# Two products of the mixing stage on GpSimd: the decay matrix times the B-C scores, and the normalisation of the probabilities

## The chip, the core and the metric

One core of a Trainium2 chip runs the whole program. The metric is the device time of one execution in microseconds (us); a kernel's time is the median of several executions. Engines are named as in the profile: PE is TensorE (matmuls; PEld its weight loads), DVE is VectorE, ACT is ScalarE, POOL is GpSimd, SP is SyncE, which issues most DMAs. L12 is line 12 of the kernel.

## What is computed

Two layers of a decoder trunk on 256 positions of width 1024. Each layer has a SwiGLU feed-forward half step, a mixing block, a second half step and a gated input embedding. The mixing block projects the normalised input and runs three branches: sparse attention over keys that an indexer picks, a pooling mixer, and a state-space scan in chunks of 128 (SSD). The two places that matter here, cut from the reference:

```python
# attention: per query block and head
logits = jnp.where(valid, q_lat @ c_sel * (HEAD_DIM ** -0.5), -jnp.inf)
probs = jax.nn.softmax(logits, axis=-1)

# SSD: per chunk, group and head
L = jnp.exp(segsum(A))                 # decay from position s to l, 0 above the diagonal
cb = jnp.einsum("bclgn,bcsgn->bgcls", Cc, Bc)
y_diag = jnp.einsum("bgecls,bcsgep->bclgep", cb[:, :, None] * L, X)
```

The normalisation of `probs` by its row sums is one of the two products, `cb * L` the other.

## The kernel before

Matmuls of float32 are done in three passes: each operand is split into a rounded high part and the rest. A weight tile of 128x1024 arrives by DMA on SP's queue as `raw` (4 buffers); ACT rounds it to `whi` (L145, 5 buffers); DVE subtracts, `wlo` = `raw` - `whi` (L146, 5 buffers); PE multiplies high by high, high by low and low by high (L211, L212, L213). Tiles are loaded in one fixed order, up to four ahead of the one in use, so ACT and DVE prepare weights all the time beside whatever else they do.

The mixing block (`mix`) writes its branches as generators and interleaves them with `weave`, which calls each generator in turn so that PE always has projection matmuls (the three branch gates `gates`, the pooling inputs) between the short steps of attention and SSD. A step of PE that needs a result is put some turns behind the step that makes it (the bare `yield`s). This gives the program order. The tile framework then plans the order of each engine's instructions by a timeline of its own (`schedule_with_timeline_sim=True` in `program`), except where the kernel fixes it (`keep_in_program_order` in `mm` and `transpose`, an order token in `turn`). So a change of an engine for some instructions can alter the order of others too. Waits between engines are semaphores, set by the framework from the tiles that are read and written.

The SSD branch (`ssd`) goes over 2 groups of 8 heads (g) and 2 chunks (h). For each it makes two tiles `m` of 128x512, four heads each (q): a scan on DVE adds up the decay rates (L1099), ACT takes the exponential (L1104), for h = 0 DVE copies the last column to `e0` (L1107), and DVE multiplies `m` by the masked scores `cb`, the same for the four heads (L1108). After three yields eight matmuls read the two tiles (`near`), in the profile `aux<-ct,ul`. That is four pairs of products per layer.

In attention, `softmax` works on two PSUM tiles of 128x512 at a time: four heads of 128 keys (first half of the queries), or two heads of 256 keys. For each head DVE adds the mask and takes the row minimum of the negated logits (L921); ACT takes the exponential and its row sum (L923); DVE takes the reciprocals (L925); ACT multiplies each head by its own (L927, four or two instructions per tile). After some yields PE transposes the probabilities (L114, `aux<-ident,t`), ACT copies them out of PSUM (L939), and the value matmuls read them. There are three rounds per layer, six tiles.

Other instructions that the prediction names: L1085, POOL's product of the SSD inputs with dt; L1030 and L1031, small DVE steps of dt; L1168 and L1169, DVE's sliding sums of the pooling branch; L1183, POOL's low part for one of the four pooling groups; L1153, DVE's multiply by the gate of SSD. The tiles of one tag share a name in the profile: `ct` is `m`, `gl` holds `cb` among others, `t` the probabilities.

Of the kernel before, what the change touches and what calls it, by code (L numbers as in the profile page):

```python
# [13 lines left out]
OP = mybir.AluOpType  # L14
AX = mybir.AxisListType

P = 128
# [51 lines left out]
class Builder:  # L69
# [838 lines left out]
    def softmax(self, h, two, mb, out):  # L908

        nc = self.nc  # L910
        nb = h + 1
        nk = nb * P
        per = 512 // nk
        prs = []
        for ps, _ in two:
            pr = self.t([P, per, nk])
            mx = self.t([P, per], tag="mx", bufs=2)
            sums = self.t([P, per], tag="sum", bufs=2)
            for j in range(per):
                x = mx[:, j:j + 1]  # L920
                nc.vector.tensor_tensor_reduce(pr[:, j], ps[:, j * nk:(j + 1) * nk], mb[:, :nk],  # L921
                                               1.0, 3.0e38, OP.add, OP.min, accum_out=x)
                self.last = nc.scalar.activation(pr[:, j], pr[:, j], AF.Exp, bias=x, scale=-1.0,  # L923
                                                 accum_out=sums[:, j:j + 1])
            nc.vector.reciprocal(sums, sums)  # L925
            for j in range(per):
                nc.scalar.mul(pr[:, j], pr[:, j], sums[:, j:j + 1])  # L927
            prs.append(pr)
            yield
        for _ in range(4 - h):  # L930
            yield
        pts = [self.bank("aux") for _ in prs]
        for pt, pr in zip(pts, prs):
            for j in range(4):
                self.transpose(pt[:, j * P:(j + 1) * P],
                               pr[:, j // nb, (j % nb) * P:(j % nb + 1) * P], self.ident)
        for (_, heads), pt in zip(two, pts):
            th = self.t([P, 4, P])
            nc.scalar.copy(th, pt.rearrange("p (a b) -> p a b", a=4))  # L939
            out.append((heads, th))  # L940
            yield
# [63 lines left out]
    def ssd(self, layer, sm, xs, xt, bc, cb, zs, room):  # L1005
        nc = self.nc
# [53 lines left out]
        def rate(*key):  # L1060
            i = wanted.index(key)
            for k in wanted[i:i + 3]:
                if k not in rates:
                    rates[k] = fetch(*k)
            return rates[key]
# [26 lines left out]
        for g in range(2):  # L1092
            gs = slice(g * 4, (g + 1) * 4)
            for h in range(2):
                ms = self.a([P, 2, 4, P], F, "ct")
                for q in range(2):

                    m = ms[:, q]
                    nc.vector.tensor_tensor_scan(m.rearrange("p a b -> p (a b)"),  # L1099
                                                 rate(g, h, q).rearrange("p a b -> p (a b)"),  # L1100
                                                 self.after.rearrange("p a b -> p (a b)"),
                                                 0.0, OP.add, OP.mult)
                    yield
                    self.last = nc.scalar.activation(m, m, AF.Exp)  # L1104
                    if h == 0:
                        k = g * 8 + q * 4
                        nc.vector.tensor_copy(e0[:, k:k + 4], m[:, :, P - 1])  # L1107
                    nc.vector.tensor_tensor(m, m, cb[:, h, g, None].to_broadcast([P, 4, P]),  # L1108
                                            op=OP.mult)
                    yield  # L1110
                ps = self.bank("aux")

                def near():
                    for j in range(8):
                        b, k = (j % 2) * 64, j // 2
                        self.mm(ps[b:b + 64, k * P:(k + 1) * P],
                                         xt[:, h, g * 8 + j], ms[:, j // 4, j % 4],
                                         start=True, stop=True)

                yield  # L1120
                yield
                yield near
                yk = y[:, gs, h * P:(h + 1) * P]
                nc.vector.tensor_tensor(yk, yk, ps.rearrange("p (a b) -> p a b", a=4), op=OP.add)
                yield

            x0 = self.t([P, 8, 64])
            nc.vector.tensor_tensor(x0, xt[:, 0, g * 8:(g + 1) * 8],
                                    e0[:, g * 8:(g + 1) * 8, None].to_broadcast([P, 8, 64]),
                                    op=OP.mult)  # L1130
            po = self.bank("aux")
            e1 = self.t([P, 4, P])
            x = rate(g, 1, 2)
            for j in range(4):
                nc.vector.tensor_tensor_scan(e1[:, j], x[:, j], self.ones, 0.0, OP.add, OP.mult)
            self.last = nc.scalar.activation(e1, e1, AF.Exp)
            yield
            yield
            for j in range(4):
                a = x0[:, 2 * j:2 * j + 2].rearrange("p a b -> p (a b)")  # L1140
                self.mm(po[:, j * P:(j + 1) * P], a, cb[:, 2, g], start=True, stop=True)
            yield
            nc.vector.tensor_tensor(e1, po.rearrange("p (a b) -> p a b", a=4), e1, op=OP.mult)
            yk = y[:, gs, P:]
            nc.vector.tensor_tensor(yk, yk, e1, op=OP.add)
            yield
            if g == 0:
                ysh, ysl = [], []
            ysh.append(self.a([P, 4, S], FR, "a4", 7))
            ysl.append(self.a([P, 4, S], FR, "a4", 7))  # L1150
            for i in range(4):
                k = g * 4 + i
                nc.vector.tensor_tensor(y[:, k], y[:, k], zs[:, k], op=OP.mult)  # L1153
                self.square(k, y[:, k])
                self.split_scaled(ysh[g][:, i], ysl[g][:, i], y[:, k],
                                  self.col(layer, "ssd_norm", k))
                yield
# [336 lines left out]
```

## Time and profile before

| | |
|---|---|
| median of 3 executions | 1299.63 us (1299.38 to 1300.03) |
| profiled execution | 1300.84 us, span 1299.1 us |
| granted PE clock | 1.0 throughout |
| DMA | 250.51 MB, mean 193 GB/s |
| POOL instructions | 27 |

The span is the time from the first to the last instruction of the profiled execution; its device time is 1.74 us longer. An engine's busy time is a sum over instructions, and matmuls overlap each other in the pipeline. In a row of a timeline the first number is the start, the second the duration of the piece, both in us; a bracket gives the idle time before it on its engine, and what ended that. A row of waits reads: engine and line that waited, engine and line waited for, us in total, times, longest. A row for a line gives durations in ns as minimum, median and maximum.

### The profile page before, as it was taken

How to read it: one execution, taken by the hardware profiler on the slowest of the kernel's cores; microseconds unless marked ns; L12 is line 12 of the kernel's file. 1: busy time of each engine (PE TensorE's matmuls, PEld its weight loads, DVE VectorE, ACT ScalarE, POOL GpSimd, SP SyncE). 2: the span in 40 equal slices, each digit the busy share in tenths (PEclk: the TensorE clock that was granted, in tenths of full speed). 3: DMA queues.
4: the chain of work that ended last, by engine and by line, in shares of the span. 5: the costliest groups of instructions: out<-in, count | busy, mean ns of one | idle time of the engine just before them, and what ended most of it. 6: DMA issues, size and time to landing. Idle time of an engine off the chain costs nothing.

```text
span 1299.1 us, 28286 instructions
## 1 busy us (share of the span) xinstructions
PE 1290.3 (99%) x11398; PEld 1282.0 (99%) x11398; DVE 1046.3 (81%) x1935; ACT 739.5 (57%) x1209; POOL 17.9 (1%) x27
## 2 busy tenths in 40 slices
PE   9999999999999999999999999999999999999998
PEld 9999999999999999999999999999999999999998
DVE  7877669987999887766997776799879989777667
ACT  6644446666874555544654444476667646544455
POOL 0000000000000000000000000000100000000000
PEclk9999999999999999999999999999999999999999
DMA  7766646586647576666556665556965566655661
GB/s 251 247 193 195 194 158 211 179 222 205 188 142 235 162 227 194 195 191 194 188 195 194 194 196 191 162 192 184 212 224 165 183 199 211 197 195 193 194 194 66
DMA packets 89571, 250.51 MB, mean 193 GB/s; under 512 B 25184, under 2 KB 27872, under 8 KB 89440
## 3 DMA queue, kind: packets, MB, share of 16 engines
q1 hardware_dynamic: 89008, 247.92, 60.6%
q8 instruction: 89, 1.46, 0.5%
q10 hardware_dynamic: 432, 0.79, 0.2%
q14 instruction: 42, 0.34, 0.1%
HBM read 245.50 MB, written 1.08 MB: 190 GB/s over the span
## 4 chain that ended last, share of the span: by engine, by line
PE 87%; DVE 7%; ACT 2%; DMA 2%; issue 2%; DVEq 0%; SPq 0%; ACTq 0%
PE mm L213 27%; PE mm L212 27%; PE mm L211 27%; DVE wlo L146 2%; DVE ct L1099 1%; PE aux L111 1%; ACT whi L145 1%; DMA gh<-rates 1%; DMA raw<-in_w_dram 1%; PE mm L230 1%; PE mm L227 1%; PE aux L213 1%; PE aux L212 1%; ACT t L923 1%; PE mm L225 1%
## 5 line engine op out<-in xcount | busy, mean ns | idle before, releaser
L145 ACT CAST whi<-raw 128x1024 fp32r<-128x1024 f32 (+1 forms) x456 | 475.1, 1045 | 484.9 <-PE mm L212 353.8
L146 DVE TENSOR_TENSOR wlo<-raw,whi 128x1024 fp32r<-128x1024 f32 (+1 forms) x456 | 552.2, 1215 | 170.1 <-ACT whi L145 162.2
L212 PE MATMUL mm<-ul,whi 128*128 128x256 f32 x2438 | 672.0, 276 | 0.0
L213 PE MATMUL mm<-uh,wlo 128*128 128x256 f32 x2438 | 671.8, 277 | 0.0
L211 PE MATMUL mm<-uh,whi 128*128 128x256 f32 x2402 | 662.3, 277 | 0.8 <-ACT whi L145 0.8
L212 PEld LDWEIGHTS mm<-ul,whi 128*128 128x128 f32 x2438 | 457.5, 188 | 0.1
L213 PEld LDWEIGHTS mm<-uh,wlo 128*128 128x128 f32 x2438 | 457.0, 188 | 0.2
L211 PEld LDWEIGHTS mm<-uh,whi 128*128 128x128 f32 x2402 | 449.8, 188 | 2.1 <-ACT whi L145 1.2
L213 PE MATMUL mm<-gh,wlo 128*128 128x256 f32 x704 | 194.1, 276 | 0.0
L212 PE MATMUL mm<-gl,whi 128*128 128x256 f32 x704 | 194.1, 276 | 0.0
L211 PE MATMUL mm<-gh,whi 128*128 128x256 f32 x704 | 193.7, 276 | 0.0
L213 PEld LDWEIGHTS mm<-gh,wlo 128*128 128x128 f32 x704 | 132.2, 188 | 0.0
L212 PEld LDWEIGHTS mm<-gl,whi 128*128 128x128 f32 x704 | 132.2, 188 | 0.0
L211 PEld LDWEIGHTS mm<-gh,whi 128*128 128x128 f32 x704 | 131.9, 188 | 0.0
L212 PE MATMUL mm<-a,whi 128*128 128x256 f32 x256 | 70.7, 276 | 0.0
L213 PE MATMUL mm<-a,wlo 128*128 128x256 f32 x256 | 70.7, 276 | 0.0
L211 PE MATMUL mm<-a,whi 128*128 128x256 f32 x256 | 70.7, 276 | 0.0
L213 PEld LDWEIGHTS mm<-a,wlo 128*128 128x128 f32 x256 | 48.1, 188 | 0.0
L211 PEld LDWEIGHTS mm<-a,whi 128*128 128x128 f32 x256 | 48.1, 188 | 0.0
L212 PEld LDWEIGHTS mm<-a,whi 128*128 128x128 f32 x256 | 48.1, 188 | 0.0
L498 DVE TENSOR_TENSOR t<-mm,rs_r 128x256 f32<-128x256 f32 x88 | 37.3, 424 | 13.2 <-PE mm L213 13.0
L499 DVE TENSOR_TENSOR t<-t,mm 128x256 f32<-128x256 f32 x87 | 36.5, 420 | 2.6
(300 smaller groups left out, 1271.1 us busy)
## 6 DMA issues: line engine op xcount, KB each, us to landing
raw<-in_w_dram SPq DMA_DIRECT2D x446, 512.0 KB, 4.3
gh<-rates SPq DMA_DIRECT2D x16, 256.0 KB, 4.1
raw<-in_w_dram SPq DMA_DIRECT2D x8, 352.0 KB, 3.0
ul<-a SPq DMA_DIRECT2D x32, 64.0 KB, 4.8
a<-in_x_dram SPq DMA_DIRECT2D x3, 512.0 KB, 5.3
gh<-rates SPq DMA_DIRECT2D x8, 128.0 KB, 4.5
a<-in_x_dram SPq DMA_DIRECT2D x1, 544.0 KB, 3.7
raw<-in_w_dram SPq DMA_DIRECT2D x2, 256.0 KB, 4.4
```

The costliest lines, as they stand in the source:

```text
L111: self.tc.keep_in_program_order(self.nc.tensor.matmul(*args, **kw))
L145: nc.scalar.copy(hi[:, :n], raw[:, :n])
L146: ins = nc.vector.tensor_tensor(lo[:, :n], raw[:, :n], hi[:, :n].bitcast(F), op=OP.subtract)
L211: (self.mm if keep else mm)(ps, a[0], b[0], start=start, stop=False)
L212: mm(ps, a[0], b[1], start=False, stop=False)
L213: mm(ps, a[1], b[0], start=False, stop=stop)
L225: (self.mm if keep and k == 0 else mm)(ps, w[0][:, s], u[0][:, k], start=k == 0, stop=False)
L227: mm(ps, w[0][:, s], u[1][:, k], start=False, stop=False)
L230: mm(ps, w[1][:, k * P:(k + 1) * P], u[0][:, k], start=False, stop=k == last)
L498: ins = [nc.vector.tensor_tensor(t, p1[0], r, op=OP.mult), nc.vector.tensor_tensor(g, t, p1[1], op=OP.mult)]
L499: nc.vector.tensor_tensor(g, t, p1[1], op=OP.mult)]
L923: self.last = nc.scalar.activation(pr[:, j], pr[:, j], AF.Exp, bias=x, scale=-1.0, accum_out=sums[:, j:j + 1])
```

## The change

Both products are given to POOL. In `softmax` one product per tile takes the place of four or two ACT multiplies: the reciprocals are spread over the keys by a stride of zero. In `ssd` only the engine changes. Nothing else in the code differs.

```diff
@@ softmax
             nc.vector.reciprocal(sums, sums)
-            for j in range(per):
-                nc.scalar.mul(pr[:, j], pr[:, j], sums[:, j:j + 1])
+            nc.gpsimd.tensor_tensor(pr, pr, sums[:, :, None].to_broadcast([P, per, nk]), op=OP.mult)
             prs.append(pr)
@@ ssd
                         nc.vector.tensor_copy(e0[:, k:k + 4], m[:, :, P - 1])
-                    nc.vector.tensor_tensor(m, m, cb[:, h, g, None].to_broadcast([P, 4, P]),
+                    nc.gpsimd.tensor_tensor(m, m, cb[:, h, g, None].to_broadcast([P, 4, P]),
                                             op=OP.mult)
```

## The prediction

> **What bounds the kernel now.** I read the page first (busy times, then the chain that ended last), then the waits of PE, then the busy time of each engine in stretches of the mixing stage, where both edits lie, and last the timeline of one stretch, engine by engine.
>
> ```profile
> span 1299.1 us, 28286 instructions
> PE 1290.3 (99%) x11398; PEld 1282.0 (99%) x11398; DVE 1046.3 (81%) x1935; ACT 739.5 (57%) x1209; POOL 17.9 (1%) x27
> PE 87%; DVE 7%; ACT 2%; DMA 2%; issue 2%; DVEq 0%; SPq 0%; ACTq 0%
> ```
>
> PE works through the whole span: 1299.1 - 1290.3 leaves 8.8 us in which it does nothing. Taking work off DVE or ACT can only give back what PE waits for them. The waits of PE and its weight loads that bear on this change are these three:
>
> ```profile
> PE mm L211 <- ACT whi L145: 0.8, 2, 0.5
> PE aux L114 <- ACT t L927: 0.8, 2, 0.4
> PEld mm L212 <- POOL t L1183: 0.4, 2, 0.2
> ```
>
> The mixing stage of each layer is the one place where DVE is full (columns: PE, PEld, DVE, ACT, POOL busy):
>
> ```profile
> 289.00:369.00 80.00, 79.35 (x740) 76.66 (x738) 69.53 (x154) 58.10 (x124) 6.13 (x5) 1.00 0.60 190
> 930.00:1010.00 80.00, 79.58 (x731) 77.12 (x731) 70.84 (x160) 57.77 (x124) 6.89 (x6) 1.00 0.63 197
> ```
>
> PE idles 0.65 us in the first of these stretches and 0.42 us in the second, 1.07 us together: all that the stage can give back, apart from small gaps between pipelined matmuls. DVE has 80 - 69.53 = 10.5 us free in the first one, but not evenly: in its middle it has none.
>
> ```profile
> 329.00:359.00 30.00, 30.00 (x298) 28.94 (x298) 29.97 (x66) 23.34 (x50) 1.22 (x1) 1.00 0.61 186
> ```
>
> **What is removed and added.**
>
> ```profile
> L1108 DVE TENSOR_TENSOR ct<-ct,gl x16: 684/692/699, 306.9 to 1002.5; 128x512 f32<-128x512 f32 x16
> L927 ACT ACTIVATE t<-t,sum x32: 389/450/507, 325.2 to 1005.1; 128x128 f32<-128x128 f32 x16, 128x256 f32<-128x256 f32 x16
> L925 DVE RECIPROCAL sum<-sum x12: 154/165/179, 323.2 to 1004.0; 128x2 f32<-128x2 f32 x8, 128x4 f32<-128x4 f32 x4
> L1085 POOL TENSOR_TENSOR ul<-ul,dt x8: 1036/1038/1905, 289.6 to 936.6; 128x512 f32<-128x512 f32 x8
> ```
>
> DVE loses 16 x 0.692 = 11.1 us, ACT 32 x 0.450 = 14.4 us. One reciprocal goes with one tile of probabilities, so POOL gains 12 products beside the 16: 28, or 14 per layer. L1085 is the same work, a product of 128x512 with a broadcast factor, on POOL already: 1.038 us at the median, so 29.1 us in all. POOL is idle 98% of the span, so its own time is no bound; the questions are when each product ends, and what its maximum of 1.905 us means:
>
> ```profile
> 289.60 4.91 POOL L1085 TENSOR_TENSOR ul<-ul,dt 128x512 f32<-128x512 f32 x4 [22.69 <-DMA raw<-in_w_dram]
> 289.27 0.19 DVE L1030 SCALAR_TENSOR_TENSOR dt<-dt_y,dt_x 128x32 f32<-128x32 f32 x1
> 289.38 1.23 DVE L146 TENSOR_TENSOR wlo<-raw,whi 128x1024 fp32r<-128x1024 f32 x1
> 290.52 1.03 DVE L1031 SCALAR_TENSOR_TENSOR da<-dt,al 128x32 f32<-128x32 f32 x1
> 937.17 1.58 DVE L146 TENSOR_TENSOR wlo<-raw,whi 128x1024 fp32r<-128x1024 f32 x1 [1.37 <-ACT whi L145]
> ```
>
> Four products at 1.038 would take 4.15 us and took 4.91: the first waited some 0.8 us, about until L146 ended. Then L1031, the size of L1030, took 1.03 us instead of 0.19, as long as a product; and the L146 at 937.17, under the end of the other four products, took 1.58 instead of 1.23. All of these read two SBUF tensors. So a POOL product and such a DVE instruction exclude each other, each way, for up to a whole instruction. [...]
>
> What it costs DVE, per layer: 8 x 0.692 = 5.5 us freed; at most 14 x 1.038 = 14.5 us blocked, at least nothing (products that run beside DVE instructions with one input from PSUM, or beside idle DVE). That is -5.5 to +9.0 us against 10.5 us free per stage. In the full middle stretch, which two pairs of products fall into (two of L1108, two normalisations), it is 1.4 us freed against 0 to 4.2 us blocked. L146 and L1099, both with two SBUF inputs, hold about half of DVE there:
>
> ```profile
> 329.00:359.00 30.00, 10.51 (x9) 1.00 0.61 186
> 329.00:359.00 30.00, 4.78 (x4) 1.00 0.61 186
> ```
>
> (L146, then L1099.) (10.51 + 4.78) / 29.97 = 51%; so I take 2.1 us blocked, 0.7 us net. I cost this at nothing on PE, because weights are prepared ahead:
>
> ```profile
> ACT whi L145 <- PE mm L212: 353.8, 249, 3.3
> 323.92 1.03 ACT L145 CAST whi<-raw 128x1024 fp32r<-128x1024 f32 x1
> 325.00 0.39 PE L211 MATMUL mm<-uh,whi 128*128 128x256 f32 x1 [0.27 <-ACT whi L145]
> 325.16 2.45 ACT L927 ACTIVATE t<-t,sum 128x128 f32<-128x128 f32 x8
> ```
>
> ACT mostly waits for PE to give a weight buffer back, so the lead is usually all the buffers. But at 325.0 the lead was used up (whi ended at 324.95, PE had waited for it). Where that happens again, lateness on DVE goes one to one to PE, and the load of the next raw tile, which waits for L146 too, comes later by as much. The multiplies that leave ACT (the eight from 325.16 to 327.6, and later ones) let the next whi start earlier, which is what pays for the 0.7.
>
> **Who waits for the products.** L1108 feeds the near-diagonal matmuls (aux<-ct,ul). The rows below are those matmuls as a group, the third of a layer's four pairs of products with its reader, and the second product of the first pair.
>
> ```profile
> L111 PE MATMUL aux<-ct,ul x64: 272/273/324, 312.4 to 367.8; 128*64 128x128 f32 x64
> 341.06 0.69 DVE L1108 TENSOR_TENSOR ct<-ct,gl 128x512 f32<-128x512 f32 x1
> 350.53 1.09 PE L111 MATMUL aux<-ct,ul 128*64 128x128 f32 x16
> 308.81 0.69 DVE L1108 TENSOR_TENSOR ct<-ct,gl 128x512 f32<-128x512 f32 x1
> 353.87 1.22 POOL L1183 TENSOR_TENSOR t<-t,t 128x256 fp32r<-128x256 f32 x1 [59.36 <-ACT t L1181]
> ```
>
> The third pair ends 8.8 us before its reader. The thinnest cover is the first pair's: it ends at 309.5, and the first such matmul is at 312.4, 2.9 us later. On POOL the product is 0.35 us longer and may stand 1.2 us behind an L146: 1.6 of the 2.9 us, so I cost it at nothing. It also waits now for ACT's Exp and, in the first half of the sequence, for DVE's copy of the last column, each by a signal from another engine. If a second such wait eats the cover, 0.5 to 1 us reach PE. Behind a waiting L1108 on POOL stand the normalisations and one L1183 per layer, whose reader waits 0.2 us already; at 353.87 it falls between two pairs, so nothing is added.
>
> The normalisation has no cover in its last round, which is where PE waits today:
>
> ```profile
> 356.32 0.63 ACT L1104 ACTIVATE ct<-ct 128x512 f32<-128x512 f32 x1 [2.52 <-DVE ct L1099]
> 355.00 2.34 DVE L1099 TENSOR_TENSOR_SCAN ct<-gh,after 128x512 f32<-128x512 f32 x2
> 357.30 0.43 DVE L1169 TENSOR_TENSOR t<-gl 128x271 f32<-128x271 f32 x1
> 357.64 0.42 DVE L921 CUSTOM_DVE_ANT_0 t<-aux,idxw 128x256 f32<-128x256 f32 x1
> 361.39 1.71 ACT L927 ACTIVATE t<-t,sum 128x256 f32<-128x256 f32 x4
> 361.52 0.16 DVE L925 RECIPROCAL sum<-sum 128x2 f32<-128x2 f32 x1
> 361.59 1.21 DVE L146 TENSOR_TENSOR wlo<-raw,whi 128x1024 fp32r<-128x1024 f32 x1
> 361.29 0.28 PE L211 MATMUL mm<-uh,whi 128*128 128x256 f32 x1
> 361.95 0.44 PE L114 MATMUL aux<-ident,t 128*128 128x128 f32 x2 [0.38 <-ACT t L927]
> ```
>
> PE stands from 361.29 to 361.95, 0.55 us over the usual 0.11 from one matmul to the next, until the first multiplies are done. Now: (1) two ACT multiplies, half of 1.71 = 0.85 us, become one product of 1.04: +0.2. (2) The first L1108 product is ready after the Exp that ends at 356.95; the scans hold the port until about 357.3; then POOL and L1169 (two SBUF inputs) come at once. If POOL goes first, L1169 and the row maxima L921 behind it, and so the whole softmax, come 1.0 later; if DVE goes first, 0. (3) The second product meets L146 at 361.59: 0 to 0.7 (what is left of 1.21 when the reciprocal and its signal are through and the first product is done). So the transposes move by -0.55 (the multiplies leave ACT, and the planner puts the products early enough) up to 0.2 + 1.0 + 0.5 = +1.7 us. I take 0.2 + 0.5 (the middle of a question that the trace leaves open) = +0.7 per layer, 1.4 us in all. In the first round two products, 2.1 us, stand in for the eight multiplies that took 2.45 from 325.16: 0. [...]
>
> **Sum.** The profiled execution took 1300.84 us, its span 1299.1, 1.21 above the median of the runs (1299.63). 1299.1 + 1.4 = 1300.5 for the span, 1302.2 for that execution, and 1299.63 + 1.4 = **1301.0 us** as a median. That is +0.11%. What this kernel's measurement can tell from no change is about 0.2%, 2.6 us.
>
> **Rivals.**
> 1. *Slower: the shared port makes DVE late where it is full.* For it: the 1.03 us of L1031; 29.97 of 30 us; the lead that was zero at 325.0. Against it: ACT loses 7.2 us per layer, 5.5 us leave DVE, and lead is usually there. Price per layer: the last normalisation at its upper end, 1.7, and of the full stretch's net at the upper end (4.2 - 1.4 = 2.8 us) 0.8 to 1.7 reaching PE as late L146: 2.5 to 3.4, in all +5.0 to +6.8, 1304.6 to 1306.4. It decides from 1.3 us per layer on.
> 2. *The end is met earlier.* The planner lays every engine's order out anew, and the products stand early enough that PE waits neither for a normalisation nor for whi: the 1.07 us of idle PE go, 1298.6. It is no change that can be measured. A gain beyond 2.6 us would need closer packed matmuls as well; nothing in the waits offers it.
> 3. *The change doesn't do what it says*: not here. Both operands lie in SBUF, and the engine is named in the call.
>
> **How the numbers follow.** No measurable change (the forecast with rival 2): 0.55, own range 1298.5 to 1302.2. Rival 1: 0.40, since two bounded terms need only half of their upper ends to pass 2.6 us together. Faster by over 0.2%: 0.05. The range from 1298.5 to 1306.5 takes in rival 2's 1298.6 and rival 1's upper 1306.4; beyond are products blocked more often than I can count here.
>
> **What would show it.** Right: POOL at about 17.9 + 29 = 47 us or more, products of 1.04 us alone and 1.5 to 2.2 under DVE; DVE instructions of two SBUF inputs (L1169, L1153, L146) lengthened by up to 1 us; the wait of the transposes now on POOL (the product stands on line 926 there, and L1108 on 1107), 0.5 to 2 us per layer; PE still at about 1290 busy. Wrong on rival 1's side: new waits of PE for L146 or L145 in 329 to 380. Wrong as a whole: PE waiting for the near-diagonal products, or PE's time between the mixing stages changed.

## The result, and the profile after

The kernel after takes 1311.52 us (median of 5, 1310.55 to 1313.61), the kernel before beside it 1299.54 (median of 5, 1299.38 to 1300.03): a ratio of 1.0094 [1.008, 1.0108] (in brackets the 95% interval), 12.0 us slower, and above the predicted range. The two profiled executions, 1311.52 and 1300.84 us, differ by 10.7 us, and so do their spans, 1309.8 and 1299.1: the loss lies within the span. The page of the kernel after, its first lines and the shares of the chain:

```profile
span 1309.8 us, 28294 instructions
...
PE 1292.7 (99%) x11398; PEld 1282.5 (98%) x11398; DVE 1055.4 (81%) x1919; ACT 729.8 (56%) x1177; POOL 58.0 (4%) x55
...
PE 91%; DVE 5%; DMA 1%; ACT 1%; issue 1%; POOL 0%; DVEq 0%; ACTq 0%; POOLq 0%
```

PE now does nothing for 1309.8 - 1292.7 = 17.1 us, 8.3 more than before; its busy time, whose ends are modelled, is 2.4 us longer. (Busy time here is the time in which at least one instruction of the engine runs; what overlaps counts once. It is not a sum over instructions.) The second thing to see is DVE: it lost 16 products, 11.1 us, and yet its busy time rose from 1046.3 to 1055.4. ACT is 9.7 us lighter, and the kernel is slower all the same. The mixing stages, one window per layer (columns: PE, PEld, DVE, ACT, POOL busy), first before, then after:

```profile
285.00:375.00 90.00, 89.35 (x827) 86.66 (x826) 79.13 (x173) 63.82 (x133) 6.13 (x5) 1.00 0.62 198
930.00:1020.00 90.00, 89.58 (x830) 86.95 (x829) 80.25 (x176) 65.24 (x139) 6.89 (x6) 1.00 0.62 195
```

```profile
285.00:375.00 90.00, 85.54 (x787) 82.10 (x786) 80.27 (x160) 58.39 (x115) 25.84 (x19) 1.00 0.58 186
930.00:1020.00 90.00, 84.72 (x764) 81.37 (x763) 80.29 (x161) 57.91 (x116) 27.28 (x20) 1.00 0.57 185
```

PE's idle time in them went from 0.65 + 0.42 = 1.07 us to 4.46 + 5.28 = 9.74: all of the new idle time lies here, at a granted clock of 1.00 as before. What PE waited for in the kernel after:

```profile
PE aux L114 <- POOL t L926: 7.6, 7, 1.7
PE mm L212 <- POOL t L1182: 1.7, 2, 0.8
...
PE mm L211 <- ACT whi L145: 0.2, 1, 0.2
```

The transposes wait for the normalisation, now on POOL, seven times, 7.6 us in all; the pooling matmuls wait for the low part that POOL makes (L1182 here, L1183 before) 0.8 us per layer. Weights, the worry of the first rival, are late once, by 0.2 us.

Why both are late is seen in the last round. The timeline of the kernel after, POOL, DVE and PE:

```profile
359.65 2.85 POOL L1107 TENSOR_TENSOR ct<-ct,gl 128x512 f32<-128x512 f32 x2 [1.95 <-ACT ct L1103]
...
357.63 2.33 DVE L1098 TENSOR_TENSOR_SCAN ct<-gh,after 128x512 f32<-128x512 f32 x2
...
359.93 1.42 DVE L1168 TENSOR_TENSOR t<-gl 128x271 f32<-128x271 f32 x1
361.27 0.41 DVE L921 CUSTOM_DVE_ANT_0 t<-aux,idxw 128x256 f32<-128x256 f32 x1
...
364.12 0.82 DVE L1167 COPY t<-t 128x8 f32<-128x8 f32 x1
...
364.97 0.66 PE L114 MATMUL aux<-ident,t 128*128 128x128 f32 x4 [1.22 <-POOL t L926]
...
366.53 0.66 PE L114 MATMUL aux<-ident,t 128*128 128x128 f32 x4 [0.55 <-POOL t L926]
```

The scans end at 359.96; POOL's decay products, begun at 359.65 (2.85 us for the two, against 2 x 1.038 = 2.08), go first, and the window sum L1168 lasts 1.42 us, where L1169, the same instruction, took 0.43 before. The four row maxima (from 361.27), then the exponentials, the reciprocals and the normalisation stand behind it. PE waits 1.22 + 0.55 us, where it waited 0.38 before.

In the middle of the stage two pairs of products and a train of four gate multiplies alternate. First the train in the kernel before, then the rows of the kernel after:

```profile
343.12 1.43 DVE L1153 TENSOR_TENSOR uh<-uh,gl 128x256 f32<-128x256 f32 x4
```

```profile
341.08 3.00 POOL L1107 TENSOR_TENSOR ct<-ct,gl 128x512 f32<-128x512 f32 x2 [15.13 <-DVE e L1106]
344.03 2.40 POOL L926 TENSOR_TENSOR t<-t,sum 128x512 f32<-128x512 f32 x2
...
342.96 4.09 DVE L1152 TENSOR_TENSOR uh<-uh,gl 128x256 f32<-128x256 f32 x4
...
356.56 1.15 POOL L1182 TENSOR_TENSOR t<-t,t 128x256 fp32r<-128x256 f32 x1 [10.12 <-ACT t L1180]
...
357.76 0.38 PE L212 MATMUL mm<-t,whi 128*128 128x256 f32 x1 [0.83 <-POOL t L1182]
```

The four multiplies took 1.43 us before (as L1153) and take 4.09 now. From there to 355.9 DVE stands for no more than 0.04 us at a time, so these 2.66 us are not made up for, and the pooling chain is late with them: DVE makes its y (L1175), ACT casts it (L1180) and POOL subtracts from it (L1182), and PE waits 0.83 us for that. In e14 below, which has the same orders and no POOL products that read whole tiles, this wait is gone.

And the first round of the kernel after, which the prediction had at nothing, on POOL, DVE and PE:

```profile
318.72 2.93 POOL L1107 TENSOR_TENSOR ct<-ct,gl 128x512 f32<-128x512 f32 x2 [6.40 <-ACT ct L1103]
...
318.95 1.20 DVE L1167 COPY t<-t 128x2 f32<-128x2 f32 x1
...
320.44 0.26 DVE L921 CUSTOM_DVE_ANT_0 t<-aux,idxw 128x128 f32<-128x128 f32 x1
...
323.91 2.04 POOL L926 TENSOR_TENSOR t<-t,sum 128x512 f32<-128x512 f32 x2 [2.26 <-DVE sum L925]
...
325.00 0.66 PE L114 MATMUL aux<-ident,t 128*128 128x128 f32 x4 [1.61 <-POOL t L926]
```

A copy of two columns takes 1.20 us where it took 0.14 before (at 318.39), since a POOL product runs; the row maxima start behind it, and PE waits 1.61 us for the first normalised tile. How much of that wait is the copy's doing is seen only in e14: without blocking, 1.25 us of it stay. In the second layer there is one thing more: POOL's scaling of the indexer's weights (L1257) comes just ahead of the normalisation, and waits for a DMA. The reciprocal is ready at 970.51, the normalisation starts at 971.89.

```profile
971.07 0.85 POOL L1257 TENSOR_SCALAR idxw<-idxw 128x256 f32<-128x256 f32 x1 [2.75 <-DMA idxw<-in_gn_dram]
971.89 3.02 POOL L926 TENSOR_TENSOR t<-t,sum 128x512 f32<-128x512 f32 x2
...
972.98 0.66 PE L114 MATMUL aux<-ident,t 128*128 128x128 f32 x4 [1.65 <-POOL t L926]
...
974.96 0.66 PE L114 MATMUL aux<-ident,t 128*128 128x128 f32 x4 [0.73 <-POOL t L926]
```

The costliest groups of POOL in the kernel after show that the blocking goes both ways:

```profile
L1107 POOL TENSOR_TENSOR ct<-ct,gl 128x512 f32<-128x512 f32 x16 | 25.9, 1634 | 72.1 <-DVE e L1106 42.4 <-ACT ct L1103 16.7 <-PE mm L213 12.8
L926 POOL TENSOR_TENSOR t<-t,sum 128x512 f32<-128x512 f32 x12 | 14.4, 1212 | 5.7 <-DVE sum L925 5.7
```

Against 1.038 us alone, 16 x (1.634 - 1.038) + 12 x (1.212 - 1.038) = 11.6 us in which POOL stood behind DVE.

### The profile page after: what moved, and what is told of

Same layout as the page of the kernel before. It is cut to its first block, busy times and chain, and to the rows that moved or that the text cites. A ratio compares the mean times of both kernels' runs of the same rounds, so it can differ in the third digit from the quotient of the medians.

```text
span 1309.8 us, 28294 instructions
## 1 busy us (share of the span) xinstructions
PE 1292.7 (99%) x11398; PEld 1282.5 (98%) x11398; DVE 1055.4 (81%) x1919; ACT 729.8 (56%) x1177; POOL 58.0 (4%) x55
## 4 chain that ended last, share of the span: by engine, by line
PE 91%; DVE 5%; DMA 1%; ACT 1%; issue 1%; POOL 0%; DVEq 0%; ACTq 0%; POOLq 0%
PE mm L213 28%; PE mm L212 28%; PE mm L211 28%; PE aux L111 2%; DVE wlo L146 2%; DVE ct L1098 1%; DVE t L1168 1%; PE aux L213 1%; PE aux L212 1%; PE aux L211 1%; ACT whi L145 1%; PE mm L230 1%; PE mm L227 1%; PE mm L225 1%; DMA gh<-rates 0%
## 5 line engine op out<-in xcount | busy, mean ns | idle before, releaser
L145 ACT CAST whi<-raw 128x1024 fp32r<-128x1024 f32 (+1 forms) x456 | 475.4, 1045 | 490.0 <-PE mm L212 374.3
L146 DVE TENSOR_TENSOR wlo<-raw,whi 128x1024 fp32r<-128x1024 f32 (+1 forms) x456 | 551.7, 1214 | 168.6 <-ACT whi L145 160.1
L498 DVE TENSOR_TENSOR t<-mm,rs_r 128x256 f32<-128x256 f32 x88 | 37.2, 423 | 13.2 <-PE mm L213 12.9
L893 POOL TENSOR_SCALAR_AFFINE_SELECT gl<-gl 128x128 f32<-128x128 f32 x4 | 2.9, 718 | 809.9 <-DVE gl L889 809.9
```

Source lines behind the costliest of these rows:

```text
L145: nc.scalar.copy(hi[:, :n], raw[:, :n])
L146: ins = nc.vector.tensor_tensor(lo[:, :n], raw[:, :n], hi[:, :n].bitcast(F), op=OP.subtract)
L498: ins = [nc.vector.tensor_tensor(t, p1[0], r, op=OP.mult), nc.vector.tensor_tensor(g, t, p1[1], op=OP.mult)]
```

## The experiments

Three theories run through the expectations. *The port*, a name only, since no run shows what in the chip does it: a POOL product and a DVE instruction that read SBUF shut each other out, as the rows above are read (L1168 1.42 us for 0.43), DVE's instructions stand behind POOL's, and what follows on DVE comes late. *The order*: with two instructions on another engine the planner lays out PE, DVE and ACT anew, and the new order is worse by itself. *The product itself* (the hand-off, in the expectations): it is longer than ACT's or DVE's, or comes through more signals, and its reader waits for just that. Experiments that add lines shift the line numbers; the instruction is named each time. Ratios are to the kernel before on the same chip.

**e1, e2: one product each.** Of the two edits of the change, e1 makes that in `ssd` only, e2 that in `softmax` only.

> Only the decay product is on POOL; the normalisation stays on ACT. Theory A (port: a POOL product blocks DVE instructions with two SBUF inputs, and the row maxima behind them come late): the blocked instruction ahead of the row maxima stays, about 1.0 us in two of the three softmax rounds of each layer, and the transposes now wait for ACT's multiplies by about that much more: +3 to +5 us over before. Theory B (hand-off: PE reaches the transposes before a product on POOL, started by DVE's reciprocal, can be ready): no normalisation on POOL, no such wait: 0 to +1.5 us.

> Only the normalisation is on POOL; the decay product stays on DVE. Theory A (port): six products per layer instead of fourteen, and they come after the row maxima, not ahead of them: +1 to +4 us. Theory B (hand-off): nearly all of the loss stays, +8 to +11 us, as waits of the transposes for POOL.

e1: 1.0019 [1.001, 1.0028], +2.5 us; e2: 1.0042 [1.0027, 1.0057], +5.5 us. Together 8, not 12: the parts don't add up to the whole. In e1 the waits of PE are still those of before, grown: the transposes for ACT's multiplies 2.7 us (0.8 before), though nothing of the softmax was moved. So the decay product alone makes the softmax late, which speaks for the port, but neither size is one that a theory gave (+3 to +5 or at most +1.5 for e1, at most +4 or at least +8 for e2).

**e3: the normalisation as one DVE product per tile,** nothing on POOL.

```diff
-            for j in range(per):
-                nc.scalar.mul(pr[:, j], pr[:, j], sums[:, j:j + 1])
+            nc.vector.tensor_tensor(pr, pr, sums[:, :, None].to_broadcast([P, per, nk]), op=OP.mult)
```

> Neither product is on POOL: the normalisation is one DVE product of 128x512 per tile (about 0.69 us, six per layer) instead of ACT's multiplies; the decay product stays on DVE. Both theories: within 1 us of before, since no POOL product blocks anything and the product follows the reciprocal on the same engine; a loss of over 3 us would say that taking the multiplies off ACT is itself the harm, by another order of PE.

1.0063 [1.0048, 1.0078], +8 us, a miss. The waits of e3 show a place that the edit doesn't touch:

```profile
PE mm L211 <- ACT t L1180: 6.1, 2, 3.0
```

The pooling branch's y stands behind the two scans in DVE's new order (y at 356.79, the scans from 354.54 for 2.33 us). So a planned order can cost 8 us with no product on POOL at all, and the order theory had to be taken seriously.

**e4: the transposes two turns later** in the kernel after, so that the normalisation has time.

```diff
-            self.weave((states(), 55, 1), (attend(), 36, 1), (pools(), 22, 0.88), (gate, 48, 1.1),
+            self.weave((states(), 55, 1), (attend(), 42, 1), (pools(), 22, 0.88), (gate, 48, 1.1),
...
-        for _ in range(4 - h):
+        for _ in range(6 - h):
```

> The changed kernel with the transposes two more turns behind the normalisation in every round. Theory B (hand-off): the waits of the transposes for POOL (7.6 us of PE in the changed kernel) go, the 2.1 us for the pooling group's low part on POOL stay: +1 to +4 us over before. Theory A in its wide form (DVE as a whole is made late, and with it the weights): PE waits for weight parts instead, +5 us or more.

1.0132 [1.0114, 1.015], +17 us: neither. The pace of the whole branch changed, the transposes waited 6.1 us and the pooling matmuls for ACT's cast 5.6 us. It tells the theories not apart; but more distance is no cheap cure.

**e5: the port alone.** The kernel before, whole; after each DVE decay product POOL makes two products of 128x256 from the same tiles into a buffer that nothing reads. No engine's order differs from before's, nothing waits for POOL's new work.

```diff
+                    for i in range(0, 4, 2):
+                        nc.gpsimd.tensor_tensor(
+                            self.t([P, 2, P], mybir.dt.bfloat16, tag="scr", bufs=1), m[:, i:i + 2],
+                            cb[:, h, g, None].to_broadcast([P, 2, P]), op=OP.mult)
```

> The kernel before, with PE's order unchanged, and after each decay product (still on DVE) two POOL products of 128x256 that read the same tiles into a scratch tile which nothing reads: about 1.04 us of POOL per decay product, 16.6 us in all, on which nothing of PE waits. Port theory: DVE instructions with two SBUF inputs that meet them are lengthened by 0.5 to 1.0 us each, and the time rises by 1 to 4 us, at the transposes of the last round and at the pooling group's low part. Order theory (the loss is where PE's planned order puts its waiting matmuls): within 0.5 us of before.

1.0076 [1.0059, 1.0094], +10 us, nearly the loss of the whole change, from work that nobody needs, and more than the port theory's 1 to 4. The page of e5, and its waits of PE:

```profile
PE 1291.4 (99%) x11398; PEld 1282.4 (98%) x11398; DVE 1058.7 (81%) x1935; ACT 740.3 (57%) x1209; POOL 56.2 (4%) x59
```

```profile
PE mm L211 <- ACT whi L145: 3.0, 2, 1.6
PE mm L212 <- POOL t L1187: 1.8, 2, 0.9
PE aux L114 <- ACT t L927: 1.6, 2, 0.8
...
```

DVE has before's instructions in before's order, and 12.4 us more of busy time. At this place it is the weights (L145) that come late, as the first rival had it, and again the pooling chain and the softmax. No engine waits for the scratch products.

**e6, e7, e8: the matmuls of the second weave in program order,** so that the planner can't move them: before, after, and e3 on such a base.

```diff
-        mm = self.nc.tensor.matmul
+        mm = self.mm if self.fix else self.nc.tensor.matmul
...
+        self.fix = True
         with self.tc.issue_after(self.last.ins):
             self.weave((states(), 55, 1), (attend(), 36, 1), (pools(), 22, 0.88), (gate, 48, 1.1),
                        apart=(0, 1))
+        self.fix = False
```

> The kernel before with all matmuls of the second interleaved part of the mixing stage fixed in program order. The base for the two next runs. Expected within 5 us of before; no theory says which way.

> The changed kernel with the same order of PE as the run before. Order theory: with PE's order the same, the change costs less than half of its 12 us, 0 to +5 us against the run before. Port theory in its wide form: the lateness of DVE is the loss, +8 to +13 us against the run before.

> The normalisation as one DVE product per tile, decay product on DVE, with the same order of PE as the two runs before. Order theory: the 8 us that this normalisation cost with its own planned order shrink to 0 to +2 us against the fixed kernel before. If instead DVE's extra 0.69 us per tile is the cause, +6 us or more stays.

1.0153 [1.0136, 1.017], 1.0184 [1.0168, 1.0199] and 1.0194 [1.0175, 1.0213]: the base lost 20 us by itself (its transposes wait 12.9 us for ACT's multiplies), and on it the change costs 3.5 us, the DVE product 4.5. A base with stalls of its own can hide others, so nothing is drawn from these three runs.

**e9 to e12: PE in a planned order that is given.** A first build records the order in which the planner puts PE's instructions; the kernel proper gets it as edges that order and don't wait. e9 is after in before's PE order, e10 before in after's, e11 is e3 in before's, e12 is e9 with the decay product in four.

```diff
+                for x, y in zip(turns, turns[1:]):
+                    tc.add_manual_dep(by[traced[y]], traced[x],
+                                      mybir.DependencyInfo(mybir.DependencyClass.NoSync,
+                                                           mybir.DependencyReason.DATA),
+                                      reason="order")
...
-                    nc.gpsimd.tensor_tensor(m, m, cb[:, h, g, None].to_broadcast([P, 4, P]),
-                                            op=OP.mult)
+                        for i in range(4):
+                            by.tensor_tensor(m[:, i], m[:, i], cb[:, h, g], op=OP.mult)
```

(The second part is e12's.)

> The changed kernel with all matmuls of PE in exactly the order that they have in the kernel before; the other engines' orders stay planned. Order theory (about half of the loss is that the new plan puts the first round's transposes 2.2 us of PE work earlier): +4 to +7 us over before instead of +12. Port theory alone: +10 to +13, as the run with idle-handed POOL products in the old order, +10.

> The reverse: the kernel before (DVE product, ACT multiplies) with PE's order taken from the changed kernel. Order theory: the transposes of the first round are met 2.2 us too early by PE, and ACT's multiplies end no sooner: +3 to +6 us. Port theory: no new POOL product, 0 to +1.5 us.

> The normalisation as one DVE product per tile, the decay product on DVE, PE's order exactly that of before. With its own plan this cost 8 us, 6 of them PE's wait for the pooling group's high part from ACT (L1180). Order theory: 0 to +2 us. If another order of ACT and DVE is what makes that part late, +6 us or more stays.

> As the changed kernel in PE's old order, but each decay product is issued on POOL as four products of 128x128, so that the read port is held for about 0.3 us at a time and DVE can go between. Port theory: DVE instructions are lengthened by 0.3 instead of 1.0 us, and 2 to 5 us of what is left over before go. If the loss is only the hand-off from DVE to POOL to PE, the time is that of the changed kernel in the old order, within 1 us, or longer by the four starts per product.

e9: 1.0065 [1.0052, 1.0077], +8.3 us, between the two expectations. e10: 1.0091 [1.0078, 1.0105], +12, above both: in after's PE order ACT's multiplies are too late, 9.2 us of waits. That looked like the order's own cost, but it is not to be added: after's order asks for the probabilities earlier, and is made for products that come earlier. e11: 1.0092 [1.0078, 1.0106], +12, with 7.6 us of waits for the pooling cast, so DVE's order, which was still free, had moved. It also shows that e9 fixed too little. e12: 1.0078 [1.0064, 1.0092], +9.8, 1.5 us more than e9 and not the gain that smaller pieces were to bring. Its group on POOL, and the row of its line:

```profile
L1115 POOL TENSOR_TENSOR ct<-ct,gl 128x128 f32<-128x128 f32 x64 | 42.1, 690 | 68.2 <-PE mm L214 42.5 <-ACT ct L1108 12.9 <-DVE e L1111 12.7
L1115 POOL TENSOR_TENSOR ct<-ct,gl x64: 446/558/1512, 308.2 to 1013.1; 128x128 f32<-128x128 f32 x64
```

A quarter took 0.69 us, not a quarter of 1.6, and the 64 hold POOL for 42.1 us instead of 25.9; a normalisation stood behind them, and its transposes waited up to 3.3 us. The shortest quarter took 0.446 us, and 30 of the 64 took at most 0.468; so about 0.46 us is taken for a quarter that nothing blocks, against 1.038 / 4 = 0.26, and the rest of the 0.69 for blocking. (One-column products in e14 took 0.19 us at the least.) Four pieces cost POOL more than one, blocked or not.

**e13 to e16: all three orders given, and POOL that only writes.** The remaining question was whether the port costs 12 us, or the port some and the order the rest. e13 is after with PE, DVE and ACT in before's order. e14 (after's orders) and e15 (before's) put in the place of each POOL product a product of one column, which keeps the signals, and two fills of the tile with a constant, so that neither product is computed; a one-column product and its fills take at least 0.19 + 2 x 0.53 = 1.25 us, more than the 1.038 of a product alone. e16 is the control of e5: the whole computation in before's orders, and a one-column product and four fills of a scratch tile in place of the two scratch products.

```diff
+    def write_only(self, x, y, z=None):
+        nc = self.nc
+        one = x[:, :1, :1]
+        self.move(nc.gpsimd.tensor_tensor(one, one if z is None else z, y, op=OP.mult))
+        for _ in range(2):
+            self.move(nc.gpsimd.memset(x, 0.001))
```

> Both products on POOL, and PE, DVE and ACT each in exactly their order of the kernel before, less the instructions that moved. Port theory: +6 to +10 us over before, as the changed kernel in PE's old order (+8.3) and the POOL products that nothing waits for (+10). Order theory in its wide form (the orders of DVE and ACT are the rest): 0 to +3 us.

> The changed kernel with PE, DVE and ACT in exactly its orders, but each POOL product is left out: in its place POOL makes a product of one column, which keeps the waits, and writes the tile twice with a constant, reading nothing. (Neither the decay matrix times scores nor the normalised probabilities are computed.) Port theory: DVE is no longer lengthened, and the loss falls from 12 to 0 to +4 us. Order or hand-off theory: PE still stands at the transposes, +8 us or more.

> The same writes in place of the products (which are left out), with PE, DVE and ACT in their orders of the kernel before. Neither port nor order: what is left is the hand-off and POOL's time. Port theory: -1.5 to +1 us. Hand-off theory: +3 us or more, as waits of PE for POOL.

> The control of the run with POOL products that nothing waits for: after each decay product (on DVE) POOL makes a product of one column and writes a scratch tile of 128x256 four times, reading nothing; all engines in the order of before, whose whole computation stays. Port theory: within 1 us of before instead of +10. If POOL's being busy, or its signals, is the cause and not its reads, +5 us or more.

| orders of PE, DVE, ACT | POOL reads | POOL only writes |
|---|---|---|
| after's own plan | after: 1.0094 [1.008, 1.0108] | e14: 1.0007 [0.9998, 1.0015] |
| before's, products moved | e13: 1.0035 [1.0022, 1.0047] | e15: 0.9989 [0.998, 0.9997] |
| before's, scratch work added | e5: 1.0076 [1.0059, 1.0094] | e16: 0.9997 [0.9989, 1.0006] |

Each row is one pair of equal orders, and in each the loss goes when POOL stops reading. POOL is busy nearly as long: 55.3 us in e14 against 58.0, of which 11.6 were spent behind DVE. e14, e15 and e16, at +0.9, -1.4 and -0.4 us, came out as the port theory had them. e13, at +4.5, lies between its two expectations: of port and order neither is the whole. The third theory, the product itself, is answered by e15: the same signals, a tile that is ready no earlier than a product alone would make it, and no loss.

The columns tell what the orders do. Where POOL only writes, after's plan costs 2.5 us over before's orders (the medians 1302.0 of e14 and 1299.43 of e15, on one chip); PE still stands at the transposes of the first round in both layers, 1.25 and 1.00 us, since in after's order they come 20 and 13 matmuls earlier than in before's:

```profile
PE aux L125 <- POOL t L101: 2.2, 2, 1.3
```

Where POOL reads, the same difference of orders costs 7.7 us (1.0094 against 1.0035). So the plan is a small cause by itself, and it makes the blocking cost more.

The pages of e14 and e16:

```profile
PE 1288.9 (99%) x11398; PEld 1281.5 (99%) x11398; DVE 1037.9 (80%) x1919; ACT 729.0 (56%) x1177; POOL 55.3 (4%) x111
```

```profile
PE 1290.1 (99%) x11398; PEld 1282.1 (99%) x11398; DVE 1046.1 (81%) x1935; ACT 739.2 (57%) x1209; POOL 47.2 (4%) x107
```

e16's DVE has 1046.1 us, before's 1046.3: its fills lengthen DVE's busy time by nothing. After and e14 have the same DVE instructions in the same order, so 1055.4 - 1037.9 = 17.5 us is what the reads lengthened DVE by (slightly more, since e14's fills lengthen two copies by 0.4 us each). Who paid is read from the groups of DVE by form, first after, then e14 (the same instructions in the same sequence of lines):

```profile
L146 DVE TENSOR_TENSOR wlo<-raw,whi 128x1024 fp32r<-128x1024 f32 x446 | 543.2, 1223 | 164.3 <-ACT whi L145 155.8
L1098 DVE TENSOR_TENSOR_SCAN ct<-gh,after 128x512 f32<-128x512 f32 x16 | 18.8, 1210 | 7.6 <-DMA gh<-rates 7.6
...
L1152 DVE TENSOR_TENSOR uh<-uh,gl 128x256 f32<-128x256 f32 x16 | 11.1, 751 | 0.1
L1168 DVE TENSOR_TENSOR t<-gl 128x271 f32<-128x271 f32 x8 | 7.6, 951 | 0.0
...
L1175 DVE SCALAR_TENSOR_TENSOR t<-t,gl 128x256 f32<-128x256 f32 x8 | 4.8, 604 | 0.3
...
L1106 DVE COPY e<-ct 128x4 f32<-128x4 f32 x8 | 3.3, 439 | 0.0
...
L1167 DVE COPY t<-t 128x2 f32<-128x2 f32 x6 | 3.0, 502 | 0.0
```

```profile
L157 DVE TENSOR_TENSOR wlo<-raw,whi 128x1024 fp32r<-128x1024 f32 x446 | 542.8, 1222 | 169.4 <-ACT whi L156 160.8
L1116 DVE TENSOR_TENSOR_SCAN ct<-gh,after 128x512 f32<-128x512 f32 x16 | 18.8, 1210 | 7.3 <-DMA gh<-rates 4.0 <-PE aux L224 3.3
...
L1177 DVE TENSOR_TENSOR uh<-uh,gl 128x256 f32<-128x256 f32 x16 | 5.7, 420 | 0.1
L1193 DVE TENSOR_TENSOR t<-gl 128x271 f32<-128x271 f32 x8 | 3.5, 433 | 0.0
...
L1200 DVE SCALAR_TENSOR_TENSOR t<-t,gl 128x256 f32<-128x256 f32 x8 | 3.4, 424 | 0.7 <-DVE t L1197 0.5
...
L1124 DVE COPY e<-ct 128x4 f32<-128x4 f32 x8 | 1.2, 178 | 0.0
...
L1192 DVE COPY t<-t 128x2 f32<-128x2 f32 x6 | 1.0, 165 | 0.0
```

The gate multiply lost 5.4 us, the window sum 4.1, the two copies 2.1 and 2.0, the pooling y 1.4; the weights' low part, the largest user of DVE by far, 0.4 and the scans nothing. The rows of the last round above show how: POOL's product becomes ready while a long instruction runs (the scans, to 359.96), waits for its end, and the next in DVE's order (L1168) pays.

## Why the prediction was wrong, point by point

**The forecast.** Its mechanism for a loss was seen (a POOL product and a DVE instruction exclude each other: 17.5 us of DVE, 11.6 of POOL), and that mechanism stood as the first rival, behind "no change". The forecast's sum of 1.4 us failed, and the rival, which had the direction, had about half the size: 5.0 to 6.8 us against 12.0. (Its upper end takes 0.5 us for a term that the text bounds by 0.7; with 0.7 it would be 7.2.)

**The step that failed most** is "I cost this at nothing on PE, because weights are prepared ahead". It let L146 and L1099 stand for all blocked instructions because they hold half of DVE's time. In the kernel after they paid 0.4 us of 17.5. The gate multiply, the window sums, the copies and the pooling y paid, and they have no lead of several buffers: the row maxima or the pooling chain come next in the queue, and PE is at most some turns away. PE waits 7.6 us for the normalisation and 1.7 for the pooling's low part, and 0.2 for L145, the wait that was named as the rival's mark. In e5, where the products came at another place, L146 paid 3.3 of the 12.4 us (547.0 against 543.7) and PE waited 3.0 us for L145, so the path is real and only not the one taken here.

**The amount blocked.** The prediction bounded it by 14.5 us per layer and counted 2.1 in the middle stretch alone. Measured: 17.5 / 2 = 8.8 per layer, 2.66 of them by one train of gate multiplies in that stretch. (The row maxima L921, with one input from PSUM, were not lengthened: the longest took 0.419 us, 0.430 before.) The 2.1 was near; that the rest of the stage has 10.5 us free on DVE did not help, because, as the timelines above are read here, a late instruction isn't made up for by idle time that lies behind its reader.

**The last round: +0.7 taken, up to +1.7.** The wait went from 0.38 to 1.22 + 0.55 us, and to 1.27 + 0.54 in the second layer. Step (2), which the trace of before had left open, came out at its upper end: L1168 took 1.42 us. A mis-sized term; its bound held.

**The first round: 0.** PE waited 1.61 us there, and 1.65 + 0.73 in the second layer. Two products do replace eight multiplies evenly, 2.04 us for 2.45, but the prediction compared durations alone. In e14, with the same orders and no blocking, 1.25 and 1.00 us of wait stay: in the new order, 20 and 13 matmuls earlier, PE comes to these transposes before the tile is ready. The rest goes with the blocking. In layer two L1257, which stood on POOL ahead of the normalisation until 971.92, was not in the prediction's list of what stands there. All rounds together, PE waited 3.8 us per layer for the normalisation, where the text expected 0.5 to 2.

**L1183: "nothing is added".** PE waited 0.83 us per layer. The fall between two pairs of products on POOL was right; its input came late through DVE's blocked queue.

**What held.** POOL's own busy time is no bound (e14: 55.3 us of POOL and 1.0007). The decay product's readers did not wait in the kernel after. The granted clock stayed at 1.00 in the mixing stages. The second rival's size comes out when nothing is blocked (e15 gives 0.9989, 1.4 us under before), but in before's orders and with PE waiting 2.3 us for weights, 0.8 in before, so not by the mechanism that it named. One size was too large: ACT's 32 x 0.450 = 14.4 us counts overlapping multiplies twice; their busy time was 11.9 us, and ACT's fell by 9.7.

**The port.** The prediction's word stands for the exclusion that its rows show (L1031 took 1.03 us instead of 0.19); what in the chip makes it, no run shows. What the runs show is that DVE's time rises with POOL's reads: e5, where POOL reads whole tiles, and e16, where it reads one column and fills, have 1058.7 and 1046.1 us of DVE in equal orders. The prediction had the exclusion and then priced it by the wrong instructions.

**What stays open.** The size depends on the order. In before's orders (e13 against e15) the reads cost DVE 1050.8 - 1038.3 = 12.5 us and the time about 6.0; in after's plan 17.5 and 11.3; in e5 12.6 and 10.3 (the times are differences of ratios). That the plan lays the blocked instructions on the way to PE because it knows of no blocking is argued from e13 and e14, not shown by a plan that does know. After's plan without blocking is 0.9 us over before (e14, interval -0.3 to +2.0) because two things nearly cancel there: the moved work gains 1.4 us (e15), the plan loses 2.5. The 2.4 us of longer busy time of PE are not explained further than that they come with its waits.

## What to carry to other kernels

Price an offload to POOL by the DVE instructions that come next after its start, and by who reads them, not by DVE's busy sum or its largest user: here a microsecond of blocked DVE cost 0.5 to 0.8 us of time. A control in which POOL only writes, with all engines' orders given, separates the port from the hand-off in one pair of runs, and the same pair in a second order shows what the plan adds; comparing kernels whose orders the planner lays out anew (e1 to e4) separated nothing here. A train of short DVE instructions was a bad neighbour of a train of POOL products here, since they alternated: three of the four gate multiplies paid 0.84 to 0.97 us each.

## What the runs showed of the hardware that was not expected

- A DVE copy with one SBUF input was blocked too: 128x2 took 1.20 us beside a POOL product, and 0.14 without one (before's at 318.39). The prediction counted two-input instructions only.
- Fills were not free for such copies: in e14 the two copies of 128x8 took 0.56 us each on average, against 0.16 in e13. Each of the two began with a fill (at 359.70 and 1002.03) and ended just behind it. DVE as a whole was not lengthened by e16's fills (1046.1 us against 1046.3).
- A POOL fill of 128x512 took 0.527 us on average in e14, half of the product's 1.038.
